# Half-array products of three mixers issued in alternating pairs; attention takes two heads at a time; a gate product padded to 128 rows

## The chip, the cores and the metric

The kernel runs on one core of a Trainium2 chip. The metric is the device time of one execution in microseconds. Engine names in this text: PE is TensorE (matmuls), DVE is VectorE, ACT is ScalarE, SP issues the DMAs.

## What is computed

Two blocks run behind each other on 256 tokens of width 1024, all in float32. The first has two layers over a latent and a context stream; each layer's mixer has a pool, a gated linear attention (GLA) and a grouped-query attention, and an MLP follows. The second has a gated delta rule, a dilated attention and two gated MLPs. The pieces that matter here:

```python
# GLA: decays of the two directions come from a gate product of rank 16 each
la_f = log_sigmoid(r_f @ wg[0] + bg[0]) / 16;  la_b = log_sigmoid(r_b @ wg[1] + bg[1]) / 16
A = einsum('bhid,bhjd,bhijd->bhij', qc, kc, decay)          # scores within a chunk, head size 64

# grouped-query attention: 8 query heads of size 64, 2 key heads, 4 query heads to each
s = einsum('bqhgd,bkhd->bhgqk', qb, k) * 64 ** -0.5
p = softmax(s);  out = einsum('bhgqk,bkhd->bqhgd', p, v)     # k, v: 256 (context) or 512 rows
mix = concatenate([pool, gla, attention]) @ w_out

# dilated attention: three groups of 8 heads of size 64, one softmax over the three groups
```

## The kernel before, in words

Every large product is made of exact high and low parts: a weight block of 256 rows by 512 columns (512 KB, tile `raw`, three buffers) is loaded by SP, split by ACT into `hi` (line 93) and by DVE into `lo` (line 94), and enters three products with the high and low parts of the activations (`hh`, `hl`). These are the products of line 76 into the PSUM rings `ps_m` and `ps_o`, and they are what fills PE nearly all of the time. All matmuls stand on line 76 (method `mm`), so that only the tiles tell them apart.

A scheduler puts the instructions of each engine into an order before the kernel runs; PE then takes them as they stand. Three strands share the PSUM banks: m (3 banks, the large products), a (2), b (2), and one bank `ps_o`. Where a mixer's strand has to wait for ACT or DVE, the scheduler puts large products of other work between its instructions.

The attention (`attend`, lines 801 to 848) works through 16 units, one query head and one tile of 128 query tokens each. Unit by unit it issues `soft` (the score product `ps_b<-KS,qs` with all 128 rows, then `ps_b<-KL,qs` with 64 rows for the low parts of the keys; row maximum on DVE, line 817; exponential on ACT, line 819; a scale by the reciprocal of the sum), two units later `turn` (transposes, line 830, copied to `PT` on ACT, line 832), three units later `values` (`ps_o<-PT,V`: stationary operand of 64 columns, so that a head's result fills 64 of 128 output partitions; two key tiles in the context, four in the latent stream). The values of a key head and token tile gather in the one bank `ps_o`, which is then split into `hh` and `hl`. The heads of the first key head, then those of the second.

The scores of GLA (`gla_intra`) have 64 rows: for each of two heads two products (two token tiles) of 64 rows, `ps_a<-lev`, at seven levels. The gate product (`gla_gates`, `ps_a<-c_wgate`) has 33 rows: 32 of rank and one of bias. The dilated attention (`dilated`, lines 1382 to 1465) makes scores of 64 rows, `dqk`, head by head, one bank a head, and value products of 64 columns, `dPT0` to `dPT2` with `dv`, nine in a head, into that head's bank.

A float32 matmul is two instructions in the trace, a float32r one (all of the large products) or a transpose one. In this text a stretch is "half" if PE is set to 64 rows or 64 columns in it, as the trace's 64\*128 and 128\*64 say.

Of the kernel before, what the change touches and what calls it, by code (L numbers as in the profile page):

```python
# [13 lines left out]
OP = mybir.AluOpType  # L14
# [13 lines left out]
class Net:  # L28
# [72 lines left out]
    def behind(self, ins, other):  # L101
        """issues ins behind other, on their engine"""
# [3 lines left out]
    def log_tables(self):  # L106
        """the tables that serve both the exponential and the logarithm"""
# [3 lines left out]
    def proj_a(self, acts, src, done, cols=(0, 512), tags=("m",), between=None):  # L111
        """tokens on partitions: out[tok, cols] for one chunk of 512 columns"""
# [20 lines left out]
    def proj_2a(self, act, src, done, first, tail=None, tail_at=0):  # L133
        """proj_a of two chunks of columns and one stream; the first blocks of both come before the others"""
# [21 lines left out]
    def proj_b(self, acts, src, done, fts=(0, 1, 2, 3), tags=("m",), between=None):  # L156
        """features on partitions: out[feat, tok], four feature tiles a chunk, two to a bank"""
# [23 lines left out]
    def rsqrt(self, ss, n, scale, post=None, eps=EPS):  # L181
        """1 / sqrt(ss * scale + eps), times post"""
# [27 lines left out]
    def rsqrt2(self, a, b, eps, out):  # L210
        """1 / sqrt(a + eps + b) of two columns"""
# [18 lines left out]
        # (v y^2 - 3 k^2) y is -2 k^3 times the next iterate, where y is k times this one  # L230
# [16 lines left out]
    def split_scaled(self, hi, lo, src, g):  # L247
        """a factor by partition on the way"""
# [11 lines left out]
    def half_ms(self, x, junk, out):  # L260
        """half the features' part of the mean squares: (tok, token tile)"""
# [4 lines left out]
    def token_r(self, x, xs, hold=False):  # L266
        """1 / rms over features: (tok, token tile)"""
# [14 lines left out]
    def turn_part(self, xs, q):  # L282
        """two feature tiles of both token tiles, features on partitions"""
# [33 lines left out]
    def gain_t(self, x, G, final=None):  # L317
        """x times a gain by feature, features on partitions, split; the factor 1 / rms by token is left to the
        products' results. half(n) takes in 512 features; finish() returns the factor by token. final: a gain along the columns whose norm comes first"""
# [20 lines left out]
        def finish():  # L340
# [4 lines left out]
            # with r1 the first norm's factor, 1/rms of r1 * y is 1 / sqrt(r1^2 s2 + eps) = (1 / r1) / sqrt(s2 + eps / r1^2)  # L345
# [10 lines left out]
    def row(self, r):  # L356
        """a factor by token laid along the columns, the same on every partition"""
# [9 lines left out]
    def norm_early(self, streams):  # L367
        """the part of norm_t that the modulation does not enter, stream by stream"""
# [28 lines left out]
    def mod(self, l, chunks, tag="m", halves=(0, 1), raws=None):  # L397
        """512 columns of the modulation a chunk, or 256 a half, features on partitions"""
# [24 lines left out]
    def mod_gain(self, l, which, g, parts=False):  # L423
        """gain g * (1 + scale) and shift, by feature; which = 0 (mixer) or 1 (mlp)"""
# [56 lines left out]
    def w_in_steps(self, l, acts, streams, c, last_ctx=False, between=None, late=None):  # L481
        """u of the streams, in three steps; the first gives one dict a stream"""
# [4 lines left out]
        for s, u in enumerate(U):  # L487
# [9 lines left out]
            u["rT"] = m[0:33, 768:1024]  # L497
# [61 lines left out]
    def pool_mix(self, u, c, mix):  # L559
# [3 lines left out]
        # columns of the output and of the table; the first tile's tokens reach 8 rows past it, and the other way round  # L563
# [19 lines left out]
    def gla_gates(self, u, c, pair, tables=False):  # L583
        """log decays of two heads, split: (tok, token tile, direction, channel)"""
# [19 lines left out]
    def gla_exp(self, la, d, c0, n, out):  # L604
        """exp of windowed sums of log decays, channels on partitions: out (ch, token tile, column)"""
# [6 lines left out]
    def gla_intra(self, qk, la):  # L612
        """A^T[j, i] of two heads within the tiles of 128 tokens: (j, head, token tile, i)"""
# [3 lines left out]
        def scores(L):  # L617
            res = []
            for h in range(2):
                b = slice(64 * h, 64 * h + 64)  # L620
                ps = self.ps()
                for tt in range(2):
                    self.mm(ps[:, tt * 128:tt * 128 + 128], L[b, tt, 1], L[b, tt, 0], True, True)
                res.append(ps[:, 0:256].rearrange("p (t c) -> p t c", t=2))
            return res
# [24 lines left out]
    def gla_pair(self, u, c, pair, state, stream, o):  # L650
        """two heads; state: direction -> block-diagonal states (entering, and after each tile); o: output or None"""
# [79 lines left out]
    def qk_prep(self, u, c, stream, want_q=True):  # L731
        """normed (and turned) queries and keys, features on partitions"""
# [13 lines left out]
        # high and low parts of a head's queries one above the other; the other way round for the second four heads  # L746
# [44 lines left out]
    def split_stack(self, hi, lo, b, src, scale):  # L791
        """high parts of src (times a factor by row) to hi, low parts of the rows b to lo"""
# [8 lines left out]
    def attend(self, qs, c, mix, nk):  # L801
        nc = self.nc
# [3 lines left out]
        units = [(kvh, tt, g, half) for kvh in range(2) for tt in range(2) for g in range(2) for half in range(2)]  # L806
        P, po = {}, {}

        def soft(i):
            kvh, tt, g, half = units[i]  # L810
            q = qs[:, 4 * kvh + 2 * g + half, tt * 128:tt * 128 + 128]
            b = slice(64 * kvh, 64 * kvh + 64)
            ps = self.ps()
            self.mm(ps[:, 0:n], q, KS[:, kvh, 0:n], True, False)
            self.mm(ps[:, 0:n], q[b], KL[b, 0:n], False, True)
            nm, l, rl = self.small(1, "nm"), self.small(1, "l"), self.small(1, "rl")
            nc.vector.tensor_reduce(nm[:], ps[:, 0:n], axis=AX.X, op=OP.max, negate=True)
            p = P[i] = self.tmp()
            nc.scalar.activation(p[:, 0:n], ps[:, 0:n], AF.Exp, bias=nm[:], accum_out=l[:])
            nc.vector.reciprocal(rl[:], l[:])  # L820
            if c["layer"] and i % 2 == 0:
# [12 lines left out]
        def values(i):  # L834
            kvh, tt, g, half = units[i]
            if (g, half) == (0, 0):
                po[0] = self.ps("o")
# [805 lines left out]
```

## Time and profile before

| | |
|---|---|
| median of 3 runs | 1940.82 us (1940.46 to 1946.51) |
| span of the profiled execution (its own time; nothing else of it is recorded) | 1942.6 us |
| PE busy in it | 1877.5 us, 97% |
| DVE, ACT busy | 1291.0 us, 1071.4 us |
| TensorE clock granted, mean | 0.991 |
| HBM read | 302.45 MB |

The span is the time from the first to the last instruction of one execution. A PE busy time counts a matmul from its start to its modelled end, and matmuls overlap, so that the time which a matmul costs is read from the distance between starts, not from its duration.

### The profile page before, as it was taken

The numbers are of one execution on the slowest core, as the hardware profiler recorded it, in microseconds if no ns is written. First come the engines' busy times: TensorE is split into PE (matmuls) and PEld (weight loads), VectorE is DVE, ScalarE is ACT, GpSimd is POOL, SyncE is SP. The second block draws the span as 40 slices with busy tenths as digits, with TensorE's granted clock in tenths as the row PEclk, the third lists the DMA queues.
The fourth block names the chain that finished last, engine by engine and source line by source line (L and its number), as shares of the span: only waits on it lengthen the run. The fifth ranks groups of instructions, "written<-read, shape, count | busy, mean of one in ns | idle before, by whom it ended". The sixth has DMA issues, their size and how long they took to land.

```text
span 1942.6 us, 33422 instructions
## 1 busy us (share of the span) xinstructions
PE 1877.5 (97%) x12432; PEld 1581.5 (81%) x12432; DVE 1291.0 (66%) x2859; ACT 1071.4 (55%) x2090; POOL 52.4 (3%) x48
## 2 busy tenths in 40 slices
PE   7999999999999999999989999898999999999999
PEld 5776567888879898756788889897899987779997
DVE  4465467576777776665467678867766677857665
ACT  5444557655475555644565557454555556666553
POOL 0000000000000000000000000404000000000000
PEclk9999999999999999999999999999999999999999
DMA  7414771366636655456245654121466554426565
GB/s 285 143 50 140 230 241 57 98 185 190 188 121 196 190 181 180 145 157 213 86 144 188 190 178 151 57 90 63 132 186 191 188 176 158 135 77 184 185 189 158
DMA packets 89594, 305.66 MB, mean 157 GB/s; under 512 B 11270, under 2 KB 15910, under 8 KB 89432
## 3 DMA queue, kind: packets, MB, share of 16 engines
q1 hardware_dynamic: 89032, 303.08, 49.6%
q8 instruction: 97, 1.59, 0.3%
q14 instruction: 65, 0.53, 0.1%
q0 software_dynamic: 400, 0.45, 0.1%
HBM read 302.45 MB, written 1.05 MB: 156 GB/s over the span
## 4 chain that ended last, share of the span: by engine, by line
PE 85%; DVE 6%; ACT 4%; DMA 3%; issue 1%; DVEq 0%; ACTq 0%; POOLq 0%
PE ps_m L76 60%; PE ps_a L76 14%; PE ps_b L76 5%; PE ps_o L76 3%; DMA raw<-in_w_mod_dram 2%; PE ps_b L830 1%; DVE k L1196 1%; ACT gt L296 1%; DVE lo L94 1%; PE ps_b L1209 1%; PE ps_m L288 1%; PE ps_m L415 0%; ACT hh L244 0%; DMA raw<-in_gdn_w_in_dram 0%; PE ps_a L1209 0%
## 5 line engine op out<-in xcount | busy, mean ns | idle before, releaser
L93 ACT CAST hi<-raw 128x512 fp32r<-128x512 f32 (+1 forms) x944 | 575.7, 615 | 542.9 <-PE ps_m L76 296.7
L94 DVE TENSOR_TENSOR lo<-raw,hi 128x512 fp32r<-128x512 f32 (+1 forms) x944 | 635.9, 682 | 340.5 <-PE ps_m L76 207.8
L76 PE MATMUL ps_m<-hh,hi 128*128 128x256 f32 x1440 | 405.5, 282 | 8.1 <-ACT gt L296 3.6
L76 PE MATMUL ps_m<-hh,lo 128*128 128x256 f32 x1440 | 403.7, 282 | 3.5 <-DVE lo L94 3.5
L76 PE MATMUL ps_m<-hl,hi 128*128 128x256 f32 x1440 | 405.2, 282 | 0.0
L76 PE MATMUL ps_m<-hi,k 128*128 128x512 f32 x1120 | 352.3, 395 | 0.0
L76 PEld LDWEIGHTS ps_m<-hh,hi 128*128 128x128 f32 x1440 | 269.4, 187 | 14.1 <-ACT gt L296 5.6
L76 PEld LDWEIGHTS ps_m<-hh,lo 128*128 128x128 f32 x1440 | 269.0, 187 | 5.8 <-DVE lo L94 4.6
L76 PEld LDWEIGHTS ps_m<-hl,hi 128*128 128x128 f32 x1440 | 269.8, 187 | 3.2 <-issue 1.9
L76 PEld LDWEIGHTS ps_m<-hi,k 128*128 128x128 f32 x1120 | 208.6, 188 | 49.4 <-ACT gt L1083 0.5
L76 PE MATMUL ps_m<-lo,k 128*128 128x512 f32 x560 | 221.4, 395 | 0.0
L76 PE MATMUL ps_m<-hi,hh 128*128 128x512 f32 (+1 forms) x440 | 174.8, 398 | 1.0 <-ACT hi L93 0.7
L76 PE MATMUL ps_m<-lo,hh 128*128 128x512 f32 (+1 forms) x440 | 173.0, 395 | 0.1
L76 PE MATMUL ps_m<-hi,hl 128*128 128x512 f32 (+1 forms) x440 | 172.1, 392 | 0.0
L76 PEld LDWEIGHTS ps_m<-lo,k 128*128 128x128 f32 x560 | 105.1, 188 | 25.5
L76 PE MATMUL ps_a<-hh,hi 128*128 128x256 f32 (+1 forms) x360 | 100.8, 280 | 0.0
L76 PE MATMUL ps_a<-hl,hi 128*128 128x256 f32 (+1 forms) x360 | 100.6, 279 | 0.0
L76 PE MATMUL ps_a<-hh,lo 128*128 128x256 f32 (+1 forms) x360 | 100.6, 280 | 0.0
L76 PEld LDWEIGHTS ps_m<-hi,hh 128*128 128x128 f32 x440 | 82.9, 189 | 20.6 <-issue 2.1
L76 PEld LDWEIGHTS ps_m<-lo,hh 128*128 128x128 f32 x440 | 82.7, 189 | 18.1 <-issue 1.3
L76 PEld LDWEIGHTS ps_m<-hi,hl 128*128 128x128 f32 x440 | 83.1, 189 | 17.5 <-issue 1.8
L76 PEld LDWEIGHTS ps_a<-hh,hi 128*128 128x128 f32 (+1 forms) x360 | 67.0, 186 | 0.5 <-ACT hh L249 0.2
(576 smaller groups left out, 2627.5 us busy)
## 6 DMA issues: line engine op xcount, KB each, us to landing
raw<-in_w_up_dram SPq DMA_DIRECT2D x96, 512.0 KB, 4.2
raw<-in_w_down_dram SPq DMA_DIRECT2D x96, 512.0 KB, 3.7
raw<-in_w_mod_dram SPq DMA_DIRECT2D x88, 512.0 KB, 4.3
raw<-in_ffn_w_in_dram SPq DMA_DIRECT2D x88, 512.0 KB, 3.6
raw<-in_ffn_w_out_dram SPq DMA_DIRECT2D x44, 512.0 KB, 3.5
raw<-in_dil_w_in_dram SPq DMA_DIRECT2D x36, 512.0 KB, 3.5
raw<-in_w_in_dram SPq DMA_DIRECT2D x32, 512.0 KB, 3.7
raw<-in_gdn_w_in_dram SPq DMA_DIRECT2D x32, 512.0 KB, 4.2
```

The source lines that it names most:

```text
L76: self.nc.tensor.matmul(out, lhsT, rhs, start=start, stop=stop)
L93: nc.scalar.copy(hi[:, c0:c1], raw[:, i, c0:c1])
L94: ins = nc.vector.tensor_sub(lo[:, c0:c1], raw[:, i, c0:c1], hi[:, c0:c1].bitcast(F32))
L288: self.nc.tensor.transpose(ps[:, k * 256 + tt * 128:k * 256 + tt * 128 + 128], xs[tt][:, kt * 128:kt * 128 + 128], self.ident[:])
L296: self.nc.scalar.activation(f[:, k], src(k), AF.Identity, bias=sh[:, kt:kt + 1], scale=G[:, kt:kt + 1])
L830: nc.tensor.transpose(ps[:, kt * 128:kt * 128 + 128], p[:, kt * 128:kt * 128 + 128], self.ident[:])
L1196: nc.vector.scalar_tensor_tensor(y[:, sh:256], p[:, 0:256 - sh], w[:, 3 - sh:4 - sh], y[:, sh:256], op0=OP.mult, op1=OP.add)
L1209: self.nc.tensor.transpose(ps[:, h * 128:h * 128 + 128], src(h), self.ident[:])
```

## The change

Four edits, and layouts that go with them.

```diff
@@ gla_intra, scores(L)
-            for h in range(2):
-                b = slice(64 * h, 64 * h + 64)
-                ps = self.ps()
-                for tt in range(2):
-                    self.mm(ps[:, tt * 128:tt * 128 + 128], L[b, tt, 1], L[b, tt, 0], True, True)
+            pss = [self.ps() for _ in range(2)]
+            for tt in range(2):
+                for h in range(2):
+                    b = slice(64 * h, 64 * h + 64)
+                    self.mm(pss[h][:, tt * 128:tt * 128 + 128], L[b, tt, 1], L[b, tt, 0], True, True)
@@ attend
-        units = [(kvh, tt, g, half) for kvh in range(2) for tt in range(2) for g in range(2) for half in range(2)]
+        units = [(tt, j) for tt in range(2) for j in range(4)]
@@ attend, soft
-            self.mm(ps[:, 0:n], q, KS[:, kvh, 0:n], True, False)
-            self.mm(ps[:, 0:n], q[b], KL[b, 0:n], False, True)
+            pss = [self.ps() for _ in range(2)]
+            for kvh in range(2):
+                self.mm(pss[kvh][:, 0:n], q[kvh], KS[:, kvh, 0:n], True, False)
+            for kvh in range(2):
+                b = slice(64 * kvh, 64 * kvh + 64)
+                self.mm(pss[kvh][:, 0:n], q[kvh][b], KL[b, 0:n], False, True)
...
@@ attend, values
-            for kt in range(nk):
-                self.mm(o[64 * half:64 * half + 64, g * 128:g * 128 + 128], V[:, kt, kvh * 64:kvh * 64 + 64],
-                        P[i][:, kt], kt == 0, kt == nk - 1)
+            for kt in range(nk):
+                for kvh in range(2):
+                    b = slice(64 * kvh, 64 * kvh + 64)
+                    self.mm(o[b, j * 128:j * 128 + 128], V[:, kt, b], P[i][kvh][:, kt], kt == 0, kt == nk - 1)
...
-        for i in range(len(units) + 3):
-            for f, k in ((soft, i), (turn, i - 2), (values, i - 3)):
+        for i in range(len(units) + 2):
+            for f, k in ((soft, i), (values, i - 2), (turn, i - 1)):
@@ dilated, scores: by pair of heads, the two halves in turn, banks "a" and "b"
@@ dilated, values
-            po = self.ps()
+            po = self.ps("o")
             for tt in range(2):
                 for kt in range(tt + 1):
                     for g in range(3):
-                        self.mm(po[b, tt * 128:tt * 128 + 128], V[:, kt, g, h * 64:h * 64 + 64], PT[tt + kt][:, g],
-                                kt == 0 and g == 0, kt == tt and g == 2)
-            self.split_evac(hh[b, pair], hl[b, pair], po[b, 0:256])
+                        for half in range(2):
+                            h = 2 * pair + half
+                            self.mm(po[64 * half:64 * half + 64, tt * 128:tt * 128 + 128],
+                                    V[:, kt, g, h * 64:h * 64 + 64], PTs[half][tt + kt][:, g],
+                                    kt == 0 and g == 0, kt == tt and g == 2)
+            self.split_evac(hh[:, pair], hl[:, pair], po[:, 0:256])
@@ gate product: 128 rows, the rows from 33 on are zero
-        c["gate"] = self.const("wgate", [33, 512], pool=p, eng=nc.sync, src=a["w_gate"][l])
+        c["gate"] = self.const("wgate", [128, 512], pool=p, eng=nc.sync, src=a["w_gate"][l])
-            u["rT"] = m[0:33, 768:1024]
+            u["rT"] = m[:, 768:1024]
+            nc.vector.memset(U[s]["rT"], 0.0)
+            nc.vector.memset(U[s]["rT"][32:33], 1.0)
             nc.scalar.copy(U[s]["rT"][0:32], ps[0:32, 0:256])
-            nc.vector.memset(U[s]["rT"][32:33], 1.0)
```

The attention now takes a unit of two heads, one of each key head, which need the two halves of the array. Its result lands with the key heads side by side, and the rows of `w_out` are put into that order beforehand. A unit takes both banks of strand b for its scores, then both for its transposes, and its values stand ahead of the next unit's transposes in the written loop. The dilated value products go to the bank `ps_o`, two heads at a time.

What the scheduler makes of it on PE, in the second layer's latent attention. Before, one unit after another (`ps_b` the scores, `PT` with `V` the values, L830 the transposes, `ps_m` the products of w_out):

```order
L76 MATMUL ps_o_10195<-PT_10169,V_6100 64x128 x4
L76 MATMUL ps_b_10200<-KS_6098,qs_9950 128x512
L76 MATMUL ps_b_10200<-KL_6099,qs_9950 128x512
L830 MATMUL ps_b_10211<-c_ident_69,tmpb_10160 128x128 x4
L76 MATMUL ps_o_10195<-PT_10193,V_6100 64x128 x4
L76 MATMUL ps_m_10428<-lo_10432,hh_9901 128x512
L76 MATMUL ps_m_10427<-hi_10435,hh_9901 128x512
```

The same place in the change, from the scores of one unit to the values of an earlier one; `PT_10132` is of the first key head, `PT_10139` of the second:

```order
L76 MATMUL ps_b_10141<-KS_6088,qs_9942 128x512
L76 MATMUL ps_b_10141<-KL_6089,qs_9942 128x512
L76 MATMUL ps_o_10118<-PT_10132,V_6090 64x128
L76 MATMUL ps_m_10413<-hi_10417,hh_9893 128x512
L76 MATMUL ps_m_10413<-hi_10417,hl_9894 128x512
L76 MATMUL ps_b_10142<-KS_6088,qs_9942 128x512
L76 MATMUL ps_b_10142<-KL_6089,qs_9942 128x512
L76 MATMUL ps_o_10118<-PT_10139,V_6090 64x128
L76 MATMUL ps_o_10118<-PT_10132,V_6090 64x128
```

Behind the last row five more value products follow in turn. The scheduler puts one value product alone behind the first key head's scores, and the other seven of the unit together behind the second's; the two `KL` products of a unit are not next to each other.

The dilated values, first pair of heads. Before, a head's nine products stand together or with transposes (L1449) between:

```order
L76 MATMUL ps_a<-dPT0a,dv 64x128 x3
L76 MATMUL ps_a<-dPT1a,dv 64x128 x3
L76 MATMUL ps_a<-dPT2a,dv 64x128 x3
L1449 MATMUL ps_b<-c_ident,L_17618 128x128 x3
L76 MATMUL ps_b<-dPT0b,dv 64x128 x3
L76 MATMUL ps_b<-dPT1b,dv 64x128 x3
L1449 MATMUL ps_a<-c_ident,L_17619 128x128 x3
L76 MATMUL ps_b<-dPT2b,dv 64x128 x3
```

In the change, from the same place on, up to the second of 17 products that follow each other:

```order
L76 MATMUL ps_o<-dPT0a,dv 64x128
L1461 MATMUL ps_a<-c_ident,L_17605 128x128 x2
L1461 MATMUL ps_b<-c_ident,L_17604 128x128 x3
L76 MATMUL ps_o<-dPT0b,dv 64x128
L76 MATMUL ps_o<-dPT0a,dv 64x128
```

Here too one product stands alone and 17 follow together, from the two halves in turn.

## Rows read from the trace of the kernel before

**Rows 1.** The page, part 1: span; busy time of PE.

```profile
span 1942.6 us, 33422 instructions
PE 1877.5 (97%) x12432; PEld 1581.5 (81%) x12432; DVE 1291.0 (66%) x2859; ACT 1071.4 (55%) x2090; POOL 52.4 (3%) x48
```

**Rows 2.** The page, part 4: the chain that ended last, by engine.

```profile
PE 85%; DVE 6%; ACT 4%; DMA 3%; issue 1%; DVEq 0%; ACTq 0%; POOLq 0%
```

**Rows 3.** Busy times by stretch: length, PE, PEld, DVE, ACT, POOL, clock, DMA share, GB/s.

```profile
180.00:235.00 55.00, 54.53 (x442) 31.88 (x446) 22.81 (x83) 34.83 (x99) 0.00 (x0) 1.00 0.75 233
300.00:367.00 67.00, 66.46 (x460) 51.31 (x460) 40.88 (x118) 51.24 (x114) 0.00 (x0) 1.00 0.13 40
905.00:960.00 55.00, 54.28 (x334) 36.04 (x334) 25.62 (x66) 35.25 (x77) 0.00 (x0) 1.00 0.38 116
1713.00:1742.00 29.00, 28.64 (x216) 23.51 (x215) 7.84 (x18) 15.53 (x38) 0.00 (x0) 1.00 0.12 37
```

**Rows 4.** Timeline of PE in the first layer's latent attention: start, duration, instruction.

```profile
352.03 0.28 PE L76 MATMUL ps_m<-hl,hi 128*128 128x256 f32 x1
352.15 0.40 PE L76 MATMUL ps_b<-KS,qs 128*128 128x512 f32 x1
352.47 0.49 PE L76 MATMUL ps_b<-KL,qs 64*128 64x512 f32 x1
352.89 0.43 PE L76 MATMUL ps_o<-PT,V 128*64 128x128 f32 x2
353.26 0.66 PE L830 MATMUL ps_b<-c_ident,tmpb 128*128 128x128 f32 x4
353.84 0.87 PE L76 MATMUL ps_o<-PT,V 128*64 128x128 f32 x6
354.64 0.39 PE L76 MATMUL ps_m<-hh,lo 128*128 128x256 f32 x1
354.86 0.28 PE L76 MATMUL ps_m<-hh,hi 128*128 128x256 f32 x1
```

**Rows 5.** Timeline of PE in the first GLA of the context, one level's scores.

```profile
104.16 0.40 PE L76 MATMUL ps_m<-hi,hl 128*128 128x512 f32 x1
104.40 0.40 PE L76 MATMUL ps_m<-lo,hh 128*128 128x512 f32 x1
104.78 0.72 PE L76 MATMUL ps_a<-lev 64*128 64x128 f32 x8
105.43 0.50 PE L76 MATMUL ps_o<-hi,hh 128*128 128x512 f32 x1
```

**Rows 6.** Timeline of PE, products of the pool, whose 64-column halves alternate.

```profile
185.17 0.72 PE L76 MATMUL ps_b<-c_band,k 128*64 128x136 f32 x10
```

**Rows 7.** Timeline of PE, one gate product and what follows it.

```profile
122.55 0.70 PE L76 MATMUL ps_a<-c_wgate,k 33*128 33x256 f32 x2
123.18 0.49 PE L76 MATMUL ps_a<-st,qd 128*128 128x128 f32 x2
```

**Rows 8.** Timeline, dilated values: first products of two pairs, a copy on ACT.

```profile
1720.57 0.50 ACT L1451 COPY dPT2a<-ps_a 128x384 f32<-128x384 f32 x1
1720.84 0.87 PE L76 MATMUL ps_a<-dPT0a,dv 128*64 128x128 f32 x6
...
1727.55 0.87 PE L76 MATMUL ps_a<-dPT0a,dv 128*64 128x128 f32 x6
```

**Rows 9.** Timeline, DVE and ACT of one unit in the second layer's latent attention.

```profile
923.64 0.69 DVE L817 TENSOR_REDUCE nm1b<-ps_b 128x1 f32<-128x512 f32 x1 [2.12 <-PE ps_b L76]
...
924.37 0.69 ACT L819 ACTIVATE tmpb<-ps_b,nm1b 128x512 f32<-128x512 f32 x1 [0.97 <-DVE nm1b L817]
...
925.04 0.57 ACT L832 COPY PT<-ps_b 128x512 f32<-128x512 f32 x1
```

**Rows 10.** Timeline of DVE, dilated scores: two heads' bias additions.

```profile
1623.67 0.55 DVE L1425 SCALAR_TENSOR_TENSOR L<-c_negd,ps_a 128x384 f32<-128x384 f32 x1
1624.14 0.55 DVE L1425 SCALAR_TENSOR_TENSOR L<-c_negd,ps_b 128x384 f32<-128x384 f32 x1
```

More of the change, by code (lines that the diff above doesn't have):

```diff
@@ L805, in attend @@
         n = nk * 128
-        units = [(kvh, tt, g, half) for kvh in range(2) for tt in range(2) for g in range(2) for half in range(2)]
+        units = [(tt, j) for tt in range(2) for j in range(4)]
         P, po = {}, {}
         def soft(i):
[L810 to L813, printed above, removed]
-            self.mm(ps[:, 0:n], q, KS[:, kvh, 0:n], True, False)
-            self.mm(ps[:, 0:n], q[b], KL[b, 0:n], False, True)
[L816 to L821, printed above, removed]
-                nc.vector.tensor_scalar_mul(p[:, 0:n], p[:, 0:n], rl[:])
-            else:
-                nc.scalar.activation(p[:, 0:n], p[:, 0:n], AF.Copy, scale=rl[:])
@@ L826, in turn @@
-        def turn(i):
-            p = P[i]
-            ps = self.ps()
-            for kt in range(nk):
-                nc.tensor.transpose(ps[:, kt * 128:kt * 128 + 128], p[:, kt * 128:kt * 128 + 128], self.ident[:])
-            P[i] = self.tile([128, 4, 128], name="PT", bufs=3)
-            nc.scalar.copy(P[i][:, 0:nk], ps[:, 0:n].rearrange("p (k t) -> p k t", k=nk))
+            tt, j = units[i]
+            q = [qs[:, 4 * kvh + j, tt * 128:tt * 128 + 128] for kvh in range(2)]
+            pss = [self.ps() for _ in range(2)]
@@ new lines, in soft @@
+            for kvh in range(2):
[3 more added lines that the diff above has]
+                self.mm(pss[kvh][:, 0:n], q[kvh][b], KL[b, 0:n], False, True)
+            P[i] = []
+            for kvh in range(2):
+                ps = pss[kvh]
+                nm, l, rl = self.small(1, "nm"), self.small(1, "l"), self.small(1, "rl")
+                nc.vector.tensor_reduce(nm[:], ps[:, 0:n], axis=AX.X, op=OP.max, negate=True)
+                p = self.tmp()
+                P[i].append(p)
+                nc.scalar.activation(p[:, 0:n], ps[:, 0:n], AF.Exp, bias=nm[:], accum_out=l[:])
+                nc.vector.reciprocal(rl[:], l[:])
+                if c["layer"] and kvh == 0:
+                    nc.vector.tensor_scalar_mul(p[:, 0:n], p[:, 0:n], rl[:])
+                else:
+                    nc.scalar.activation(p[:, 0:n], p[:, 0:n], AF.Copy, scale=rl[:])
@@ L834, in values @@
+        def turn(i):
+            for kvh in range(2):
+                p = P[i][kvh]
+                ps = self.ps()
+                for kt in range(nk):
+                    nc.tensor.transpose(ps[:, kt * 128:kt * 128 + 128], p[:, kt * 128:kt * 128 + 128], self.ident[:])
+                P[i][kvh] = self.tile([128, 4, 128], name="PT", bufs=3)
+                nc.scalar.copy(P[i][kvh][:, 0:nk], ps[:, 0:n].rearrange("p (k t) -> p k t", k=nk))
         def values(i):
-            kvh, tt, g, half = units[i]
@@ L836, in values @@
-            if (g, half) == (0, 0):
+            tt, j = units[i]
+            if j == 0:
                 po[0] = self.ps("o")
@@ L1416, in dilated @@
                 self.proj_a([act], src[2 * g + w], done)
[L1417 to L1420 removed]
+            for pair in range(4):
+                pss = [self.ps(t) for t in "ab"]
                 for tt in range(2):
                     n = 128 * (tt + 1)
[L1423 to L1427 removed]
+                    for half in range(2):
+                        b = slice(64 * half, 64 * half + 64)
+                        self.mm(pss[half][:, 128 * tt:128 * tt + n], qk[0][b, pair, tt * 128:tt * 128 + 128],
+                                qk[1][b, pair, 0:n], True, True)
+                for half in range(2):
+                    h = 2 * pair + half
+                    nc.vector.scalar_tensor_tensor(L[h][:, g], negd[:, g], SLOPES[8 * g + h], pss[half][:, 0:384],
+                                                   op0=OP.mult, op1=OP.add)
         for g in range(3):
@@ L1455, in dilated @@
                     for g in range(3):
-                        self.mm(po[b, tt * 128:tt * 128 + 128], V[:, kt, g, h * 64:h * 64 + 64], PT[tt + kt][:, g],
-                                kt == 0 and g == 0, kt == tt and g == 2)
-            self.split_evac(hh[b, pair], hl[b, pair], po[b, 0:256])
+                        for half in range(2):
+                            h = 2 * pair + half
+                            self.mm(po[64 * half:64 * half + 64, tt * 128:tt * 128 + 128],
+                                    V[:, kt, g, h * 64:h * 64 + 64], PTs[half][tt + kt][:, g],
+                                    kt == 0 and g == 0, kt == tt and g == 2)
+            self.split_evac(hh[:, pair], hl[:, pair], po[:, 0:256])
         self.thread("m")
@@ L1601, in _layout @@
     a["g_qk_col"] = np.stack([np.stack([np.tile(q, 2), np.tile(k, 2)], 1) for q, k in zip(x["g_q"], x["g_k"])])
-    for k in ("w_out", "w_up", "w_down"):
+    heads = 512 + np.arange(512).reshape(2, 4, 64).transpose(1, 0, 2).reshape(-1)
+    a["w_out"] = np.stack([_blocks(v[np.concatenate([np.arange(512), heads])]) for v in x["w_out"]])
+    for k in ("w_up", "w_down"):
         a[k] = np.stack([_blocks(v) for v in x[k]])
```

62 lines of the change are left out of this document (27 added, 35 removed).

## The prediction, made before the changed kernel ran

> **What bounds the kernel now.** I read the page first: PE is busy for 97% of a span of 1942.6 us [rows 1], and 85% of the chain that ended last lies on it, against 10% on DVE and ACT and 3% on DMA [rows 2]. A busy share alone would not do, since overlapping matmuls count from start to modelled end. So I went to the stretches that hold the four edits: in the first layer's latent attention (300 to 367), in the second's (905 to 960) and in the dilated values (1713 to 1742) PE is busy for 66.5 of 67, 54.3 of 55 and 28.6 of 29 us, while DVE and ACT are below 80% [rows 3]. The context attention of the first layer (180 to 235) has a second limit close by: the modulation's weights keep the DMA engines at 0.75, 233 GB/s [rows 3]. So in three places a microsecond taken off PE should come out of the span, and in the fourth only in part.
>
> Next, what a half product costs PE, from distances between starts [rows 4]. Two hardware matmuls of a value product take 0.37 us up to the next instruction (352.89 to 353.26), six take 0.80 (353.84 to 354.64): four more cost 0.43, **0.108 us each**, which is 0.217 for a float32 value product. The 0.15 that is left of the pair is the price of entering and leaving. The four transposes between the two stretches take 0.58 where four such steps would be 0.43: another 0.15. And the first large product behind takes 0.22 (354.64 to 354.86), where its neighbour ahead takes 0.12 (352.03 to 352.15). So a visit to a half stretch costs 0.30 to 0.35 us beside its own work: **0.17 us for each change** between the whole array and halves, or between the two kinds of half. KS to KL to values (0.32, then 0.42) shows the same.
>
> Do two halves run at once? The pool's products show it for column halves: ten hardware matmuls of mostly 120 and 136 columns, the halves in turn, are over in 0.72 us [rows 6], where six value products' matmuls of 128 columns on one half last 0.87 [rows 4]. For row halves the level scores of GLA show it: eight matmuls of 128 columns, four of each half, take 0.65 us up to the next instruction [rows 5], against 1.02 for eight on one half (0.37 and six more at 0.108).
>
> **The change part by part.** I counted both instruction orders: PE changes its setting 533 times before and 476 times after.
>
> *Value products of the first layer's latent attention.* 64 of them, 64 × 0.217 = 13.9 us. After, two units have all eight products in turn (4 × 0.217 = 0.87) and six have one alone and seven together (5 × 0.217 = 1.08): 8.2 us. That is −5.6. Changes of setting there go from 82 to 62: −20 × 0.17 = −3.4. Together **−9.0**.
>
> *The same in the second layer.* 13.9 become 7 × 1.08 + 0.87 = 8.4: −5.4. Changes 70 to 60: −1.7. Together **−7.1**.
>
> *The context's.* 32 products, 6.9 us; one unit with four in turn (0.43) and seven with one alone and three together (0.65): 5.0, −1.9. Changes 154 to 155. With the DMA at 0.75 I let half through: **−1.0** (bounds 0 and −1.9).
>
> *Gate products.* 128 rows keep PE whole. The work of one stays (two matmuls of 256 columns, 2 × 0.216); one gate product takes 0.63 [rows 7], 0.20 more than that. In the GLA stages changes fall by 7 and 11, and by 2 in an in-projection: −20 × 0.17 = −3.4, of which I keep **−2.5**, since the second layer's lie among products that wait for modulation weights. Against it stand two longer tables, 256 KB instead of 66: 0.19 MB at 233 GB/s is 0.8 us, once at the start, where I take it that nothing hides it, once behind the MLP, whose products do: **+0.7**. The added zeroing of 128 by 256 elements on DVE needs only the tile, which is free long before the products that ACT copies into it; no more than 0.3 us each (below half of a 0.69 pass [rows 9]), four times, hidden by PE's products: 0, at most +1.2.
>
> *Level scores of GLA.* Both halves already ran at once in the old order [rows 5]. Alternating pairs change nothing in the stream: **0**. (Bounds: 0, and, for the 21 of 61 stretches that become fully alternating, the 0.37 us between 1.02 and 0.65: −8.) The Trainium skill says in "TensorE: Matmul & The Clock Gate", Part 3, "What overlaps and what doesn't", that matmuls start and end in strict program order; by that, two products on one half followed by two on the other would overlap in one step only, and this edit would be worth the full −8 us. The row of 0.65 us speaks against it, and I go by the row.
>
> *Low-part key products (KL).* In only two of 24 units do the two become neighbours: **0** beside the changes already counted.
>
> *Dilated scores.* DVE adds a bias every 0.47 us [rows 10], eight a group, 3.8 us; PE's 8 × 6 × 0.108 = 5.2 us of one-half work is 2.6 in pairs, faster than DVE takes the banks back: **0** (bounds 0 and −1 a group).
>
> *Dilated values.* A pair of heads recurs every 6.7 us [rows 8]. In it stand 18 products, 3.9 us and three visits; after, 10 × 0.217 = 2.2 and two visits, so PE could gain about 2 us a pair, 8 in all. But `PT` has one buffer a head. Before, one head's copies ran under the other's products; now all six copies of the next pair (0.48 to 0.50 each [rows 8], 2.9 us, and a split, which I put at 0.4, somewhat below a copy of more columns) come behind the shared stretch. 2.2 and 3.3, with 0.4 for leads, give a period of 5.9: −0.8 for three pairs, about −2.4, and the first pair none, for its second head's exponentials come late. **−2.4** (bounds 0 and −8).
>
> *A new wait.* A unit now needs both banks of strand b. From the first scores: 0.5 to their end, maximum 0.69, exponential 0.69, a scale no longer than that, transposes 0.58, copy 0.57 [rows 4, 9], about 3.7 us, before the bank is free for the next unit. PE's work in a unit of the second layer is two score pairs (2 × 0.74), values 1.08 and two visits 0.3, transposes 1.1, six products of 512 columns at 0.24 [rows 5]: 5.4 us. It covers the chain. The second head's transposes stand only about 2.5 us behind its scores, where the chain needs 2.6: I add 0.2 in eight units, **+1.5** (bounds 0 and +8).
>
> Sum: −9.0 −7.1 −1.0 −2.5 +0.7 −2.4 +1.5 = −19.8, hence 1942.6 − 19.8 = 1922.8 for an execution like the profiled one, which is 1.8 us above the median of the runs; against those, **1921.0**.
>
> **The rivals.**
>
> *Only the changes of setting are saved.* If halves of value products did not overlap (the pool's products have 16 to 136 columns, these have other weights at each step), 57 × 0.17 = −9.7 remains, about 1931. Rows 6 speak against it.
>
> *Strict order on PE.* As above, the level scores gain 8 us more: 1913. [rows 5] contradict it for this form, but it was read where the second half's bank was free.
>
> *The gain goes to the next wait.* ACT is busy for 51.2 of the 67 us in 300 to 367 [rows 3]; nine fewer would leave it 88% busy, and a queue in fixed order can then make PE wait. If neither this stage nor the dilated one gives anything, −19.8 + 9.0 + 2.4 = −8.4, and if the second layer's does not either, −1.3: 1939, no change.
>
> *The coupled pair makes it slower.* Mechanism: `soft` takes both banks of strand b and gets them back only from two transposes and two copies. If other strands' DVE and ACT work (passes of 512 columns, 0.69 each by [rows 9]) falls into the chain three or four times a unit, 3.7 becomes about 6.5 to 7, and PE, in fixed order, stands 1.1 to 1.6 us in each of 16 latent units: +18 to +26, less 19.8 gained: up to 1947. It decides against the change from a wait of 1.2 us a unit on. That ACT copies `PT` within 0.6 us of its transposes in the rows speaks against it.
>
> **How the numbers follow.** Forecast with its bounds, −10 to −30: 0.68. Only changes saved: 0.08. Strict order: 0.05. Given to the next wait: 0.11. Slower: 0.08. 0.3% is 5.8 us, about what a measurement of this kernel can tell from no change. Faster is the first three and a third of the fourth, 0.84; same the rest of the fourth and a little of the fifth, 0.10; slower 0.06. The range 1909 to 1937 holds the forecast with its bounds, and the first two rivals; it leaves out the no-change and the slower end.
>
> **What would show it.** In the changed profile: a stretch of eight value products in the latent attention takes some 0.6 us instead of 1.02, and one that stands alone 0.37; 16 gate products without the 0.2 of a visit; the level scores still at 0.65; a pair of dilated heads recurs in 5.9 us; the second attention ends some 7 us earlier against its start. The prediction is wrong if PE waits for ACT's `PT` or exponentials in the latent attentions (over 1 us a unit), if seven products in turn take 1.6 us, or if the copies of the dilated pairs leave PE idle for more than they save.

## The result, and the profile after

The changed kernel takes 1916.6 us (median of 4 runs, 1909.57 to 1920.99) against 1943.64 us (4 runs, 1940.46 to 1946.51) for the kernel before: ratio 0.9858, 95% interval 0.9822 to 0.9893, so 1.4% faster. The forecast was 1921, with 1909 to 1937 as its range. It was counted from 1940.82, so it foresaw a gain of 19.8 us; the medians here lie 27.0 apart.

The page of the changed kernel, its part 1 and the chain that ended last, for [rows 1, 2]:

```profile
span 1910.7 us, 33441 instructions
PE 1846.9 (97%) x12432; PEld 1558.0 (82%) x12432; DVE 1289.9 (68%) x2853; ACT 1069.2 (56%) x2080; POOL 52.3 (3%) x48
...
PE 87%; DVE 6%; DMA 3%; ACT 3%; issue 1%; DVEq 0%; ACTq 0%; POOLq 0%
```

PE has the same 12432 instructions, but 31 us less of busy time, and it is as much the bound as before. DVE and ACT did not change: what was gained is PE's own time. The busy times of the four stretches, at the places of [rows 3] (length, PE, PEld, DVE, ACT, POOL, clock, DMA share, GB/s):

```profile
180.00:235.00 55.00, 52.30 (x453) 29.66 (x455) 24.09 (x91) 33.04 (x92) 0.00 (x0) 1.00 0.76 241
300.00:357.00 57.00, 56.30 (x444) 44.42 (x443) 36.72 (x100) 46.23 (x100) 0.00 (x0) 1.00 0.17 57
888.00:938.00 50.00, 48.73 (x322) 31.20 (x323) 27.19 (x66) 35.29 (x79) 0.00 (x0) 1.00 0.32 103
1689.00:1709.00 20.00, 19.64 (x214) 16.09 (x213) 5.94 (x13) 13.74 (x34) 0.00 (x0) 1.00 0.16 54
```

In the two latent attentions and the dilated values PE is still nearly full: 56.3 of 57, 48.7 of 50 and 19.6 of 20 us. The windows are set by hand, so their lengths measure no gain; the table below does. In the context's attention PE has more room now (52.3 of 55), with the DMA engines still at three quarters.

**Where the time went.** Both kernels have the same 8968 float32r matmuls (the large products, the score products KS and KL, and sums of GLA's decays), so the start of the k-th of them in one trace can be set against the k-th in the other. The last column takes away what the clock did: in both traces the granted clock falls to 0.50, the level of 1.2 GHz, for some stretches of 3 to 7 us, at different places. A fall behind PE's last matmul is not counted. The loss is one minus the granted clock, summed over windows of 1 us; where PE would have waited anyway that takes away too much, so a net figure is sure to about 1.7 us (half of a stretch of 3.4) for each such stretch.

```
stage (us of before)                              after - before   of it clock   net
start to end of the context's GLA (0-161)              -3.3           -1.7      -1.5
context's attention and modulation (161-294)           -3.5           -3.4       0.0
latent attention, first layer (294-370)                -6.0           +1.7      -7.7
MLPs, in-projection of layer 2 (370-804)               +1.3           +1.7      -0.4
GLA and modulation, second layer (804-877)             -5.2           -3.4      -1.8
latent attention, second layer (877-964)               -6.0            0.0      -6.0
MLP to dilated scores (964-1688)                       -0.6            0.0      -0.6
dilated values (1688-1752)                             -8.6            0.0      -8.6
rest                                                    0.0            0.0       0.0
sum                                                   -31.9           -5.1     -26.8
```

The net of −26.8 lies near the difference of the medians (−27.0); the raw −31.9 of the two profiled executions is 5 us further: the one of before happened to lose 17 us to the clock, the one after 12. The two stages that carry the argument best, the second layer's latent attention and the dilated values, have no such correction at all.

**The parts, as the trace shows them.** Timeline of PE in the second layer's latent attention, one unit of two heads (start, duration, instruction); it answers to [rows 4], which are of the first layer:

```profile
901.26 0.50 PE L76 MATMUL ps_b<-KL,qs 64*128 64x512 f32 x1
901.69 0.43 PE L76 MATMUL ps_o<-PT,V 128*64 128x128 f32 x2
902.06 0.50 PE L76 MATMUL ps_m<-hi,hh 128*128 128x512 f32 x1
...
902.95 0.49 PE L76 MATMUL ps_b<-KL,qs 64*128 64x512 f32 x1
903.37 1.09 PE L76 MATMUL ps_o<-PT,V 128*64 128x128 f32 x14
904.39 0.66 PE L838 MATMUL ps_b<-c_ident,tmpb 128*128 128x128 f32 x4
```

Read the distances: the lone value product takes 0.37 us, and the seven behind it, 14 hardware matmuls, 1.02 (903.37 to 904.39), which is what eight matmuls of one half took before. In each step of 0.109 us one matmul of each half goes through. Over the three attentions the stretches of value products take 28.4 us instead of 42.0. The list of PE's waits is empty between 895 and 932.

Level scores and gate products, for [rows 5] and [rows 7]:

```profile
102.84 0.72 PE L76 MATMUL ps_a<-lev 64*128 64x128 f32 x8
103.48 0.50 PE L76 MATMUL ps_o<-hi,hh 128*128 128x512 f32 x1
```

```profile
120.39 0.65 PE L76 MATMUL ps_a<-c_wgate,k 128*128 128x256 f32 x2
120.88 0.38 PE L76 MATMUL ps_a<-st,qd 128*128 128x128 f32 x2
```

Eight level scores in full alternation take 0.64 to 0.65 us, as before. A gate product takes 0.49 where it took 0.63.

Dilated values, the first pair, PE (for [rows 8]):

```profile
1690.12 0.43 PE L76 MATMUL ps_o<-dPT0a,dv 128*64 128x128 f32 x2
...
1691.18 0.32 PE L76 MATMUL ps_o<-dPT0b,dv 128*64 128x128 f32 x1
1691.19 0.32 PE L76 MATMUL ps_o<-dPT0a,dv 128*64 128x128 f32 x1
...
1693.29 0.66 PE L1461 MATMUL ps_a<-c_ident,L 128*128 128x128 f32 x4
...
1694.93 0.43 PE L76 MATMUL ps_o<-dPT0a,dv 128*64 128x128 f32 x2
```

The two halves start 6 to 7 ns apart, 17 products are over in 2.11 us (1691.18 to 1693.29), and the next pair's first product stands 4.81 us behind that of the first. The four starts are 1690.12, 1694.93, 1699.97 and 1704.70, a mean period of 4.86 us. In the trace of before the first and the last of the four pairs start so, which makes a mean period of 6.9:

```profile
1713.87 0.87 PE L76 MATMUL ps_a<-dPT0a,dv 128*64 128x128 f32 x6
...
1734.57 0.87 PE L76 MATMUL ps_a<-dPT0a,dv 128*64 128x128 f32 x6
```

The stretches of value products take 9.9 us in all, where they took 17.5. ACT between the first two stretches of the changed kernel:

```profile
1693.71 0.48 ACT L1463 COPY dPT0a<-ps_a 128x384 f32<-128x384 f32 x1
1694.08 0.48 ACT L1463 COPY dPT1a<-ps_a 128x384 f32<-128x384 f32 x1
1694.45 0.50 ACT L1463 COPY dPT0b<-ps_b 128x384 f32<-128x384 f32 x1
1694.88 0.48 ACT L1463 COPY dPT2a<-ps_a 128x384 f32<-128x384 f32 x1
1695.25 0.49 ACT L1463 COPY dPT1b<-ps_b 128x384 f32<-128x384 f32 x1
```

The copies start 0.37 us apart (one 0.43), though each lasts 0.48 to 0.50, and they run while PE makes the next transposes. In the whole stage, 1689 to 1709, PE's list of waits has one entry (total, times, longest):

```profile
PE ps_a L1461 <- ACT dPT0a L1463: 0.3, 1, 0.3
```

The same list for before, 1712 to 1742, has one wait of 0.3 us too: PE set the pace of this stage before and after.

### The profile page after: what moved, and what is told of

It is laid out like the page before. It is cut to its first block, busy times and chain, and to the rows that moved or that the text cites. A ratio compares the mean times of both kernels' runs of the same rounds, so it can differ in the third digit from the quotient of the medians.

```text
span 1910.7 us, 33441 instructions
## 1 busy us (share of the span) xinstructions
PE 1846.9 (97%) x12432; PEld 1558.0 (82%) x12432; DVE 1289.9 (68%) x2853; ACT 1069.2 (56%) x2080; POOL 52.3 (3%) x48
## 4 chain that ended last, share of the span: by engine, by line
PE 87%; DVE 6%; DMA 3%; ACT 3%; issue 1%; DVEq 0%; ACTq 0%; POOLq 0%
PE ps_m L76 61%; PE ps_a L76 14%; PE ps_b L76 4%; PE ps_o L76 3%; DMA raw<-in_w_mod_dram 2%; PE ps_b L838 1%; DVE k L1205 1%; DVE lo L94 1%; ACT gt L296 1%; PE ps_m L288 1%; PE ps_b L1218 1%; PE ps_m L415 0%; DMA raw<-in_gdn_w_in_dram 0%; ACT hh L244 0%; PE ps_a L1218 0%
## 5 line engine op out<-in xcount | busy, mean ns | idle before, releaser
L76 PEld LDWEIGHTS ps_m<-hi,hh 128*128 128x128 f32 x440 | 82.8, 188 | 19.6 <-issue 1.0
L76 PEld LDWEIGHTS ps_m<-lo,hh 128*128 128x128 f32 x440 | 82.6, 188 | 17.1 <-DVE lo L94 0.6
```

Of the source, the lines that this page charges most:

```text
L76: self.nc.tensor.matmul(out, lhsT, rhs, start=start, stop=stop)
```

## Experiments

Theory A: a matmul on one half runs beside one on the other, wherever the two stand near each other in PE's queue, and PE sets the pace of all the stages concerned. Its rivals were a gain from fewer changes of setting alone, strict order on PE, and a gain that goes to the next wait. All ratios are against the kernel before, run on the same chip.

### One edit at a time

Each of these is the kernel before with one of the four edits of the diff, and nothing else.

**Dilated edit alone.**

> The kernel before with the dilated edit alone (scores by pair of heads, values in the shared bank, the two halves in turn). Theory A, halves run at once and the copies of PT lie beside the transposes of PE: a stretch of 17 value products takes 2.11 us as in the changed kernel, a pair of heads recurs every 4.7 to 5.4 us instead of 6.7 to 7.0, and the whole is 8 us (0.4%) faster. Theory of the prediction, copies on the path: a pair every 5.9 us, 2.4 us faster. Rival, only settings are saved (8 fewer changes at 0.17 us): 1.4 us faster, a stretch of 17 takes about 3.8 us.

Measured: ratio 0.9953 (0.9939 to 0.9968), 1930.64 us against 1940.07. Stretches of 17 products take 2.11 us, the lone products start at 1707.70, 1712.52, 1717.55 and 1722.29, a period of 4.86 us. The stage is 8.6 us shorter. The prediction's period of 5.9, and the rival that only settings are saved (1.4 us, a stretch of 3.8), are both out.

**Attention edit alone.**

> The kernel before with the attention edit alone (units of two heads, value products in turn, w_out's rows reordered). Theory A, halves run at once: seven value products in turn take 1.02 us with their visit, one alone 0.36, the two latent attentions gain 7 and 6 us and the context's about nothing, because its modulation weights bound it: 13 to 14 us (0.7%) faster in all. Rival, only settings are saved (34 fewer changes at 0.17 us): 6 us. Rival, the gain is given to a new wait on the two banks of strand b: PE is idle for more than 0.5 us a unit there and the whole gains less than 6 us.

Measured: 0.9942 (0.9926 to 0.9959), 11 us. By the same alignment, less the clock, the latent attentions are 6.6 and 5.1 us shorter, and the context's stage 2.5 (sure to 1.7). That is a little below theory A and twice what fewer settings would give.

**Gate product alone.**

> The kernel before with the gate product padded to 128 rows and nothing else. Theory: 19 fewer changes of PE's setting at 0.17 us and 0.7 us more for the longer table, so 2.5 us (0.13%) faster, all of it in the two GLA stages. Rival: the products of the padded rows cost as much as the change they save, or the zeroing on DVE is late: no difference or up to 1.2 us slower.

Measured: 0.9981 (0.9971 to 0.9991), 3.7 us (1.7 to 5.6). The gate stretches take 8.1 us instead of 10.2 in all, and by the alignment the two GLA stages are 2.0 and 0.5 us shorter; no loss for the longer table or the zeroing shows.

**Level scores alone.**

> The kernel before with the level scores of GLA in alternating pairs and nothing else; 24 of the 61 stretches alternate fully. Theory, PE overlaps halves in whatever order they stand within a stretch, if the bank is free: a stretch of eight hardware matmuls takes 0.645 us as before, and the whole stays within 0.1%. Rival, starts and ends in strict order: the old stretch would overlap in one step only, and 24 stretches gain 0.37 us each, 9 us (0.46%).

Measured: 0.9983 (0.9966 to 1.0001), by this interval not told from no change. The ten runs reach from 1931.74 to 1945.74 us, and the medians (1933.82 and 1940.07) are 6.2 us apart, so the edit as a whole may well be worth 3 to 6 us. But that gain is not made by level scores that overlap better, as strict order would have it: their stretches take 43.9 us in all, where they took 43.2. By the alignment 0.9 and 2.3 us of it lie in the two latent attentions, where the scheduler now makes eight fewer changes of setting; where the rest lies is not shown.

The four together, 0.47 + 0.58 + 0.19 + 0.17 = 1.41%, give about what the whole change gives (1.42%). The five intervals together leave some 0.45%, 9 us, either way, so that the edits helping or hindering each other by less than that is not excluded.

### How near must the halves stand, and who sets the dilated pace

**Nine and nine.** The changed kernel, with one half's nine products ahead of the other's:

```diff
-            for tt in range(2):
-                for kt in range(tt + 1):
-                    for g in range(3):
-                        for half in range(2):
...
+            seq = [(tt, kt, g) for tt in range(2) for kt in range(tt + 1) for g in range(3)]
+            for i in range(0, 9, 9):
+                for half in range(2):
+                    for tt, kt, g in seq[i:i + 9]:
...
```

> The changed kernel with the dilated value products of a pair not in turn: nine of the first half, then nine of the second, into the same shared bank. Theory, PE starts a product of the other half early only if it stands a few instructions ahead in the queue: the stretch of 15 products takes 3.2 to 3.4 us instead of 2.11 for 17, a pair of heads takes some 1.5 us longer, and as PE sets the pace there the dilated stage loses 5 to 7 us against the changed kernel. Rival one, any order overlaps while the bank is free: stretch about 2.0 us, no loss. Rival two, the copies on ACT set the pace, as the prediction had it: stretch 3.3 us, but a loss of at most 2 us in the stage.

Measured: 0.9894 (0.9865 to 0.9924). The dilated stage is 2.9 us shorter than before, not 8.6: 5.7 lost. PE's timeline of the third pair, where the first half ends:

```profile
1705.73 0.65 PE L76 MATMUL ps_o<-dPT0a,dv 128*64 128x128 f32 x4
...
1706.87 0.49 PE L76 MATMUL ps_o<-dPT2a,dv 128*64 128x128 f32 x3
1707.09 0.32 PE L76 MATMUL ps_o<-dPT0b,dv 128*64 128x128 f32 x1
1707.20 0.27 PE L76 MATMUL ps_o<-dPT2a,dv 128*64 128x128 f32 x1
...
1707.47 0.49 PE L76 MATMUL ps_o<-dPT0b,dv 128*64 128x128 f32 x3
...
1709.20 0.55 PE L1461 MATMUL ps_a<-c_ident,L 128*128 128x128 f32 x3
```

The second half does start before the first has ended, but only beside its last matmuls: three of the first half (1707.20, 1707.31 and 1707.41) start behind the second half's first. No written order alone would give that: the second half's first matmul starts between the two of one product of the first half (the third in the row of 1706.87, and 1707.20). The stretch of 34 matmuls takes 3.47 us; one by one, at 0.109 and with 0.15 for the visit, it would be 3.86. So theory A holds with a limit: it saves 3.5 steps at the border, no more (the stretches of 15, at 3.04 us instead of 3.42, say the same). The 5.7 us that come back are the 5.5 us by which the value stretches grew (15.4 instead of 9.9 in all), and nothing hid them. That fits PE as the pace. By itself it would also fit copies that follow the stretch, one behind the other; PE's list of waits above, which has 0.3 us in this kernel too, and the two buffers below put those out.

**Three and three** (the same with groups of three).

> The changed kernel with the dilated value products in turns of three (six hardware matmuls of a half at a time). In the traces of before, four of a half and then four of the other overlap fully and eight and eight hardly do. If the reach is at least six: stretches as short as with single turns and no loss against the changed kernel. If it is four: two of each six are left alone, a stretch of 15 products takes 2.3 to 2.8 us and the stage loses 2 to 4 us.

Measured: 0.9884 (0.9853 to 0.9915); stretches of 15 products take 2.11 us, one of 17 takes 2.17. The alternatives were too simple: six matmuls of a half at a time overlap in full, though at the border above only three of the first half were still to start. A reading that fits the starts, but that no run tests: each group begins beside the last three or four matmuls of the group ahead, so that both halves always have one to run. The stage loses 1.4 us against the changed kernel, because one to three products now stand alone ahead of the stretch (11.1 us of value stretches against 9.9).

**Two buffers for each PT tile of the dilated attention** (`bufs=2`).

> The changed kernel with two buffers for each of the dilated PT tiles. Theory, PE sets the pace of a pair and the copies on ACT lie beside its transposes: the dilated stage stays within 0.5 us of the changed kernel's. Rival, what the prediction took for the limit: copies that wait for the products to read PT make part of the period even now, and the stage gains 2 us or more over four pairs.

Measured: 0.9859 (0.9832 to 0.9885), 0.0001 from the changed kernel's ratio. The dilated stage is 8.7 us shorter than before, the lone products start 4.77, 5.04 and 4.73 us apart. So the buffer that the prediction saw as the limit does not set the period.

### What the lone products still cost

**Value products joined.** The first value product of a unit is issued behind the step's last KL product (`last[0]`), and the first dilated one behind the second head's last transpose. Of the edit, the part in the attention:

```diff
-                    self.mm(o[b, j * 128:j * 128 + 128], V[:, kt, b], P[i][kvh][:, kt], kt == 0, kt == nk - 1)
+                    ins = self.mm(o[b, j * 128:j * 128 + 128], V[:, kt, b], P[i][kvh][:, kt], kt == 0, kt == nk - 1)
+                    if kt == kvh == 0:
+                        self.behind(ins, last[0])
```

> The changed kernel with the lone first value product of an attention unit held back behind that step's last KL product, and the lone first dilated value product behind the second head's last transposes, so that they join the others: 29 fewer changes of setting. Theory, each lone visit costs 0.36 us and joins for nothing: 13 in the attentions and 4 in the dilated stage, 6 us faster than the changed kernel, ratio to before 0.983. Rival, holding back makes PE wait for a bank or PT: no gain or a loss of up to 0.5 us a unit, ratio 0.986 or more.

Measured: 0.9826 (0.9805 to 0.9847), 1907.74 us. Where the eight stand together they take 1.025 us, where one and seven took 0.36 and 1.02; a product still stands alone in 8 of the 24 units, where it did in 20. The dilated stage is 10.3 us shorter than before instead of 8.6; a pair recurs every 4.5 us. The interval overlaps the changed kernel's, so the 6 us between the ratios rest on these stretches and not on the totals.

**And the KL products joined:** the first KL product is issued behind the second KS product.

> As the kernel before it, and the first KL product of a unit also held back behind the second KS product, so that the two KL products of 64 rows run at once: 80 fewer changes than the changed kernel. Theory, a visit for one KL product costs 0.42 us and two together 0.43 to 0.57: 21 units by 0.3 us, another 6 us, ratio to before 0.980. Rival, the first head's softmax now starts only when both banks of strand b are free, the chain of the unit grows by 0.5 to 1 us, and PE waits for it: the latent attentions lose what they gained, ratio 0.984 or more.

Measured: 0.9815 (0.9792 to 0.9838), 1906.21 us. Between the two theories in total; by layer, each fits one. PE in the second layer's latent attention:

```profile
901.91 0.50 PE L76 MATMUL ps_b<-KS,qs 128*128 128x512 f32 x1
903.01 0.54 PE L76 MATMUL ps_b<-KS,qs 128*128 128x512 f32 x1 [0.59 <-ACT PT L842]
903.47 0.79 PE L76 MATMUL ps_b<-KL,qs 64*128 64x512 f32 x2
```

PE now waits there for the copy that frees the second bank, and the list of its waits between 895 and 932 (total, times, longest), empty in the changed kernel, begins so:

```profile
PE ps_b L840 <- ACT tmpb L828: 2.5, 4, 0.9
PE ps_b L76 <- ACT PT L842: 1.3, 3, 0.6
```

Of the 8.8 us, net of the clock, that this attention had gained with the value products joined, 4.0 are left. (At 903.3, behind these waits, the granted clock also fell to 0.50 for 3.4 us; that is taken off already.) The first layer's gains: its latent attention, with the MLP behind it that takes over some of its large products, is 12.0 us shorter than before, counted up to 514 us of the trace of before, against 8.5 without the KL edit.

**KL joined in the first layer alone.**

> The lone value products joined everywhere, the KL products joined in the first layer's attentions alone, where the run before gained by it, and left apart in the second layer's, where PE was seen to wait for PT. Theory, the two effects are of those places: the first layer keeps 19 to 20 us against before, the second layer 8 to 9, ratio to before 0.979 to 0.980. Rival, the difference in the second layer was the clock's and not the wait's: ratio 0.9815 as before or above.

Measured: **0.9773** (0.9751 to 0.9796), 1899.39 us. The interval is clear of the changed kernel's. It lies below the 0.979 to 0.980 expected; by the medians (1899.39 against 1940.85) it is 0.9786. The second layer's latent attention is 7.8 us shorter than before, with no correction for the clock, and PE no longer waits for `tmpb` or `PT` there; of the two waits that its list still has between 895 and 932 this is the longer:

```profile
PE ps_m L76 <- ACT hh L244: 0.7, 1, 0.7
```

So it was the wait, and not the clock, that had cost the gain there. In the first layer one unit now looks like this:

```profile
320.96 0.48 PE L76 MATMUL ps_b<-KS,qs 128*128 128x512 f32 x1
321.37 0.51 PE L76 MATMUL ps_b<-KL,qs 64*128 64x512 f32 x2
321.80 1.09 PE L76 MATMUL ps_o<-PT,V 128*64 128x128 f32 x16
322.82 0.38 PE L76 MATMUL ps_m<-hl,hi 128*128 128x256 f32 x1
```

Two KL products take the 0.43 us that one took, and eight value products 1.02.

## Why the prediction was right, point by point

- **The bound.** PE's time came out of the span in the latent attentions and the dilated values, as read from [rows 3]. The mechanism was right as well: two halves run at once, by the starts above and by the nine-and-nine kernel.
- **Value products and settings.** The terms for the three attentions were −9.0, −7.1 and −1.0, and +1.5 for a new wait: −15.6. Measured: −7.7, −6.0 and 0.0, so −13.7, and no wait: PE has none in the second layer's units between 895 and 932. Without the wait the terms come to −17.1, 3.4 us too large. The product part is as forecast: stretches of value products lost 13.6 us, against 12.9. What came out lower is the credit for fewer changes (−3.4 and −1.7), part of which lies within those stretches already. The context's share is not settled: the table has 0.0, sure to some 3.4 us, and the attention edit alone 2.5 us, sure to 1.7 (its term was −1.0, with bounds 0 and −1.9).
- **Gate products.** −2.5 + 0.7 was forecast; the two GLA stages show −1.5 and −1.8, and the edit alone −3.7 (−1.7 to −5.6). The 0.7 for the longer table was not seen, and is smaller than what these figures can tell.
- **Level scores: 0.** Right for the stretches, and for the reason given: halves overlap without alternation if they are as near as four and four. What the prediction did not have is that the edit moves the scheduler's order elsewhere, where 3 us or more may be gained. The rule of strict order in the Trainium skill ("TensorE: Matmul & The Clock Gate", Part 3, "What overlaps and what doesn't") is contradicted, as to starts, by the start at 1707.09 in the nine-and-nine kernel: a matmul of the second half starts ahead of three that precede it in the written order. The ends in a trace are modelled and show nothing here. So PE takes its instructions as they stand only within a half.
- **Dilated values: the step that was mis-sized.** The prediction said that "all six copies of the next pair [...] come behind the shared stretch" and that 2.2 and 3.3 with 0.4 "give a period of 5.9". Measured: 4.86, and −8.6 us instead of −2.4, just past the far bound of −8. The period of 6.7 that it started from was the shortest of three (6.97, 6.71 and 7.02). Two things more were wrong. The copies were taken at their duration (0.48), while they start 0.37 apart; and they were added to the products as if PE had nothing to do meanwhile, though the next pair's 18 transposes take 18 × 0.109 = 2.0 us of PE in any case and stand just there. PE's own work of a pair is 2.0 + 2.11 + 0.36 = 4.5 beside its re-entries, nearly the whole period. PE waits for 0.3 us in the whole stage, two buffers changed nothing, and lengthening PE's part lengthened the stage by as much: together they show that PE, not the copies, is the pace. [rows 3] had said so of the stage before (28.64 of 29 us).
- **Dilated scores and KL products: 0.** The stage that ends with the dilated scores shows −0.6; nothing speaks against either.
- **The sum.** −19.8 was forecast, −27 measured. The dilated values gave 6.2 us more than their term, the GLA stages 1.5 and the rest 1.0; the attentions gave 1.9 less. That errors of both signs met in the sum is luck, and so is part of the nearness of 1921 to 1916.6: the gain was 7 us off, the time only 4, since the kernel before ran 2.8 us slower in the comparison than the median that the forecast starts from.
- **The sign that does not fit.** For "a stretch of eight value products" the prediction names 0.6 us instead of 1.02. By its own price of 0.217 for a pair in turn, eight products take 0.87 and a visit, and 1.02 was measured; 0.6 is what eight hardware matmuls, four products, take (0.59 in the context's attention).
- **The rivals.** Saving settings alone, strict order and a coupled pair that waits are out for this kernel. The wait of the last one became real in the second layer once the KL products were coupled too, at up to 0.9 us a time; even there the attention stayed faster than before.

## What to carry to other kernels

Products that fill half of the array run two at a time if the halves stand within a few instructions of each other; strict alternation is not needed, but a block of 18 matmuls of one half followed by 18 of the other gains only a tenth (0.38 of 3.86 us). Each visit to a half setting costs here as much as a product or two (0.30 to 0.35 us, a product 0.22), so look in the scheduled order for products that stand alone, and tie them to their neighbours, but not where that holds back the head of a chain that PE is about to need: in the second layer PE then waited up to 0.9 us a time. When a wait is costed, ask what the engine that is said to wait would do meanwhile: work that it has to do anyway there is its cover.

## What the runs showed of the hardware

- **How far ahead PE starts the other half.** With 18 matmuls of a half in a row the overlap at the border was 3.5 steps of 0.109 us; with six it was complete; with eight and eight of the kernel before, 16 matmuls took 1.76 us in one place and 1.84 in another (955.43), nearly the 1.89 of one by one:

```profile
364.84 1.83 PE L76 MATMUL ps_o<-PT,V 128*64 128x128 f32 x16
366.60 0.38 PE L76 MATMUL ps_m<-hl,hi 128*128 128x256 f32 x1
```

  That is 1.2 and 0.5 steps at the border, and not 3.5. So the reach is not one fixed number; what sets it is not shown.
- **The clock.** In every profiled execution the granted clock fell to 0.50 (1.2 GHz) several times, each time behind a stretch with gaps in PE's work. Most falls lasted 3.4 or 6.8 us; the longest, in the profiled execution of the level-score edit at 242.1, 27.3 us. In the changed kernel, ahead of the first layer's latent attention (windows of 2 us; length, PE, PEld, DVE, ACT, POOL, clock, DMA share, GB/s):

```profile
290.00:292.00 2.00, 0.56 (x2) 0.30 (x2) 1.99 (x10) 1.79 (x6) 0.00 (x0) 1.00 0.00 0
292.00:294.00 2.00, 2.00 (x13) 1.53 (x13) 2.00 (x10) 1.41 (x4) 0.00 (x0) 0.73 0.00 0
294.00:296.00 2.00, 2.00 (x12) 2.00 (x11) 1.27 (x4) 1.62 (x5) 0.00 (x0) 0.50 0.25 66
```

PE was busy for 0.56 of 2 us, and at work again it got half of the clock. In the trace of before the clock did not fall there, but it fell at 865.4, in a window (864 to 866) with PE busy for 0.51 of 2 us. Which of the gaps are followed by a fall differs between kernels, and the runs of one kernel differ in it: those of the changed kernel show a mean granted clock of 0.990 (1920.99 and 1920.30 us) or 0.994 to 0.995 (1912.90 and 1909.57). So one profiled execution against another can mislead by 5 us here (−31.9 against −26.8), and a stage's difference is read only beside the clock of both.
